# Residue-ordered copies of the normalised activations as stationary operand of six projection chunks in a hybrid decoder trunk

## Chip, cores and metric

The kernel runs on one core of one Trainium2 chip. The metric is device time in microseconds (us) of one execution; lower is better. TensorE (PE) multiplies, with its weight loads recorded apart (PEld); VectorE (DVE) and ScalarE (ACT) do elementwise work, SyncE (SP) and ACT issue the transfers.

## What is computed

One decoder layer over 512 tokens of width 1024, in float32. The part that matters here: the input is normalised (`h`, 512 x 1024), multiplied by a wide matrix `w_in`, and the product is split; among the pieces are query, key and value for three attention groups whose dilation is 1, 4 and 16:

```
h = _rms(x, norm1_w[l]) * (1 + sc1) + sh1
z, xbc, dt_raw, q, k, v, u, gates = jnp.split(h @ w_in, splits, axis=-1)
...
for gi, (win, dil) in enumerate(DILATED_GROUPS):      # ((128, 1), (512, 4), (2048, 16))
    o, lse = _dilated_window_attn(qh[:, :, sl], kh[:, :, sl], vh[:, :, sl], win // dil, dil, slopes[gi])
```

For dilations 4 and 16 the kernel wants the tokens of q, k and v grouped by their residue modulo 4: 128 tokens 0, 4, 8, ..., then 1, 5, 9, ..., and so on. After attention come a state-space branch (SSD), a pooling branch, gates, output projections and an MLP.

## The kernel before

**Number format.** Every large product is made of three: both operands are split into a high part (float32r) and a low part, and `mm3` issues low x high, high x high and high x low into the same PSUM bank (lines 285, 286, 287).

**Layout of a projection chunk.** Features lie on partitions: `hh[k]` and `hl[k]` (k = 0..7) are the high and low part of 128 features by 512 tokens. A chunk is 512 output columns of `w_in`: 8 values of k, 4 blocks j of 128 tokens, 3 products, 96 matmuls. `gemm_tok` (line 301) takes 128 tokens of `hh[k]` or `hl[k]` as the stationary operand and streams the 512 weight columns `wh`, `wl`. In the names of the profile, `psacc<-wl,hh`, the moving operand comes first and the stationary one second. Its argument `mod` selects the view of the tokens: contiguous blocks of 128, or every fourth token (`toks`, line 298). `gemm_feat` (line 289) takes the weights as the stationary operand instead and streams the tokens. `wstream` loads 512 KB of weights per two k (`raw`), splits them on ACT (`wh`, line 270) and DVE (`wl`, line 271), with three buffers each.

**First stage (lines 332 to 486).** The order on DVE, ACT, PE and SP is written out by hand. Per k: SP loads 4 blocks of the modulation matrix (`wa`) and two weight blocks (`wst`); DVE makes the modulation by dot products (line 366) and the low parts of the weights (line 385); `high(k)` scales the input (ACT line 442 and DVE line 443) and writes `hh[k]` (ACT line 446); `low(k)` writes `hl[k]` (DVE line 450); `w_high` splits weights on ACT (line 381). PE runs chunks Q and K (group 0, contiguous tokens) k by k as the operands appear. Work that follows this stage may not be placed before the two instructions `edgeV` and `edgeS`.

**Middle stage.** A scheduler orders the rest. PE runs the chunks Q+1, K+1, Q+2, K+2 (all `mod=True`), VV (`mod=False`), VV+1, VV+2 (`mod=True`), and then the `gemm_feat` chunks. Between the matmuls of these chunks stand short blocks of other PE work: transposes of q and k (lines 534, 539), scores (line 555), the exchange of softmax statistics (line 596) and the transposes of the probabilities (line 652). `take`, `take_k` and `take_v` empty the PSUM banks on ACT (line 322). In the background, DVE works off 64 further modulation dot products (line 235), whose blocks `wa` SP loads.

**Memory.** All 128 x 512 blocks come from one set of 59 slots (`blk`, `free`): a freed slot goes to the end of a queue and the next request takes its head, so a new block waits for the last reader of the old one.

Of the kernel before, what the change touches and what calls it, by code (L numbers as in the profile page):

```python
# [10 lines left out]
F32 = mybir.dt.float32  # L11
F32R = mybir.dt.float32r
AF = mybir.ActivationFunctionType
# [81 lines left out]
Z, XS, BCC, Q, K, VV, U, GS, GA, GP = 0, 2, 4, 5, 8, 11, 14, 16, 18, 20  # L95
# [3 lines left out]
def kernel(ctx: ExitStack, tc: tile.TileContext, a: dict, out: bass.AP, dbg=None):  # L99
# [16 lines left out]
    class Slots:  # L116
# [6 lines left out]
        def take(self, name, dt):  # L123
            i = self.idle.pop(0)
            t = self.pool.tile([P, T], dt, tag=f"{self.prefix}{i}", name=uid(name), bufs=1)
            self.used[id(t)] = (i, t)
            return t

        def free(self, t):
            self.idle.append(self.used.pop(id(t))[0])  # L130
# [3 lines left out]
    def blk(name, dt=F32):  # L134
        return sb.take(name, dt)
# [5 lines left out]
    def small(shape, name, bufs=1, dt=F32):  # L141
        return sm.tile(shape, dt, tag=name, name=uid(name), bufs=bufs)
# [4 lines left out]
    def acc():  # L147
        return psm("acc")
# [6 lines left out]
    V, S = nc.vector, nc.scalar  # L155
# [70 lines left out]
    def ada_load(part, k):  # L226
        wa = [blk("wa") for _ in range(2)]
        for i in range(2):
            nc.sync.dma_start(wa[i], a["w_ada"][part * 8 + k][:, i * T : (i + 1) * T])
        return wa  # L230
# [31 lines left out]
    def flush():  # L262
        while side:
            side.pop(0)()
# [9 lines left out]
    def wstream(w, nk, ch, k0=0, ahead=None):  # L274
        for kp in range(nk // 2):
            with tc.high_priority(offset=AHEAD if ahead is None else ahead):
                raw = raws.tile([P, 2, T], F32, tag="raw", name=uid("raw"))
                nc.sync.dma_start(raw, w[ch, k0 // 2 + kp])
                wh, wl = wsplit(raw, [P, 2, T])
            for i in range(2):  # L280
                yield 2 * kp + i, wh[:, i, :], wl[:, i, :]
            tick()

    def mm3(ps, wh, wl, xh, xl, first, last):
        mm(ps, lhsT=wh, rhs=xl, start=first, stop=False)  # L285
        mm(ps, lhsT=wh, rhs=xh, start=False, stop=False)  # L286
        mm(ps, lhsT=wl, rhs=xh, start=False, stop=last)  # L287
# [10 lines left out]
    def toks(t, mod):  # L298
        return t.rearrange("p (j r) -> p r j" if mod else "p (r j) -> p r j", r=4)

    def gemm_tok(w, nk, ch, ah, al, mod, ahead=None):

        ps = [acc() for _ in range(4)]
        for k, wh, wl in wstream(w, nk, ch, 0, ahead):
            th, tl = toks(ah[k], mod), toks(al[k], mod)
            for j in range(4):
                mm3(ps[j], th[:, j, :], tl[:, j, :], wh, wl, k == 0, k == nk - 1)
        return ps
# [7 lines left out]
    def evac(ps, name, func=AF.Copy):  # L316

        with tc.high_priority(offset=SOON):
            xs = [blk(name) for _ in ps]
            for x, p in zip(xs, ps):  # L320
                if func is AF.Copy:
                    S.copy(x, p)
                else:
                    S.activation(x, p, func)
        free(*ps)
        return xs

    w_in = a["w_in"]
# [3 lines left out]
    with tc.manual_schedule(engines={E.DVE, E.Activation, E.PE, E.SP}):  # L332
# [4 lines left out]
        def w_load(k):  # L337
            for ch in (Q, K):
                wt[ch, k] = blk("wst")
                nc.sync.dma_start(wt[ch, k], w_in[ch, k // 2][:, k % 2, :])  # L340
# [17 lines left out]
        A1 = [small([P, 2], f"A1{k}") for k in range(8)]  # L358
# [3 lines left out]
        def dot(k, i, half):  # L362
            if (k, i) not in dots:
                dots[k, i] = small([P, 2], "dot", 4)
            x = wa[i][half]
            V.scalar_tensor_tensor(x, x, 1.0, crow[half], ALU.mult, ALU.mult, accum_out=dots[k, i][:, half : half + 1])
            free(x)

        def dot_end(k, i):
            d, o = dots[k, i], A1[k][:, i : i + 1]  # L370
            if i == 0:
                V.scalar_tensor_tensor(o, d[:, 0:1], bsc1[:, k : k + 1], d[:, 1:2], ALU.add, ALU.add)
                V.tensor_tensor(o, o, vc("norm1_w", k), ALU.mult)
            else:
                V.scalar_tensor_tensor(o, d[:, 0:1], vc("b_ada", k), d[:, 1:2], ALU.add, ALU.add)
# [3 lines left out]
        def w_high(ch, k):  # L379
            wparts[ch, k] = blk("wsh", F32R), blk("wsl", F32R)  # L380
            S.copy(wparts[ch, k][0], wt[ch, k])

        def w_low(ch, k):
            wh, wl = wparts[ch, k]
            V.tensor_tensor(wl, wt[ch, k], wh.bitcast(F32), ALU.subtract)
            free(wt[ch, k])
# [44 lines left out]
        R1 = blk("R1")  # L431
        dot(0, 1, 1)
        dot_end(0, 1)
        hh = [cpool.tile([P, T], F32R, name=f"hh{k}", tag=f"hh{k}") for k in range(8)]
        hl = [cpool.tile([P, T], F32R, name=f"hl{k}", tag=f"hl{k}") for k in range(8)]

        us = {}

        def high(k, R):
            u = us[k] = blk("u1")  # L440
            if k:
                S.mul(u, xT[k], A1[k][:, 0:1])
                V.tensor_tensor(u, u, R, ALU.mult)
            else:
                V.scalar_tensor_tensor(u, xT[k], A1[k][:, 0:1], R, ALU.mult, ALU.mult)
            return S.activation(hh[k], u, AF.Identity, bias=A1[k][:, 1:2])

        def low(k):
            u = us.pop(k)
            i = V.scalar_tensor_tensor(hl[k], u, A1[k][:, 1:2], hh[k].bitcast(F32), ALU.add, ALU.subtract)  # L450
            free(u, xT[k])
            return i

        high(0, rp)
        w_low(Q, 0)
        S.copy(R1, rp)
# [3 lines left out]
        qps = [acc() for _ in range(4)]  # L460
        kps = [acc() for _ in range(4)]
        for k in range(8):
            if k < 7:
                wa = [ada_load(1, k + 1), ada_load(0, k + 1)]
                w_load(k + 1)
                dot(k + 1, 0, 0)
                if k:
                    low(k)
                dot(k + 1, 0, 1)
                w_high(Q, k + 1)  # L470
                w_high(K, k + 1)
                dot(k + 1, 1, 0)
                dot_end(k + 1, 0)
                dot(k + 1, 1, 1)
                w_low(Q, k + 1)
                dot_end(k + 1, 1)
                edgeS = high(k + 1, R1)
                w_low(K, k + 1)
                if k == 6:
                    edgeV = low(7)  # L480
            th, tl = toks(hh[k], False), toks(hl[k], False)
            for ch, ps in ((Q, qps), (K, kps)):
                wh, wl = wparts[ch, k]
                for j in range(4):
                    mm3(ps[j], th[:, j, :], tl[:, j, :], wh, wl, k == 0, k == 7)
                free(wh, wl)
# [16 lines left out]
    def take_k(ps):  # L503
        ks, rk = take(ps, "k")
        for tb in range(4):
            kv = ks[tb].rearrange("p (h e) -> p h e", h=4)
            with tc.high_priority(offset=SOON):
                V.tensor_tensor(kv, kv, rk[:, tb * 4 : tb * 4 + 4].unsqueeze(2).broadcast_to([P, 4, P]), ALU.mult)
        return ks

    def take_v(ps):
        return evac(ps, "v")
# [433 lines left out]
    def do(gen, n):  # L946
        side.extend([pieces(gen)] * n)

    def call(f, *args):
        side.append(lambda: f(*args))  # L950

    probs, vals, stats, pTs, oh, ol = [], [], [], [], [], []
# [22 lines left out]
    def rest(n):  # L975
        side.extend([lambda: None] * n)
# [14 lines left out]
    with tc.issue_after(edgeV.ins), tc.issue_after(edgeS.ins):  # L991
        qs, rq = take(qps, "q")
        ks = take_k(kps)
        do(ssd_steps(), 5)
        scores(0, qs, rq, ks)
        qps = gemm_tok(w_in, 8, Q + 1, hh, hl, True, 0)
    for gi in (1, 2):
        if gi > 1:
            qps = gemm_tok(w_in, 8, Q + gi, hh, hl, True)
        qs, rq = take(qps, "q")  # L1000
        kps = gemm_tok(w_in, 8, K + gi, hh, hl, True)
        ks = take_k(kps)
        flush()
        rest(gi - 1)
        scores(gi, qs, rq, ks)
    vals.append(take_v(gemm_tok(w_in, 8, VV, hh, hl, False)))
    call(do_joint)
    vals.append(take_v(gemm_tok(w_in, 8, VV + 1, hh, hl, True)))
    for h in range(4):
        call(turn_head, h)  # L1010
    vals.append(take_v(gemm_tok(w_in, 8, VV + 2, hh, hl, True)))
    for h in range(4):
        call(out_head, h)
    ps = evac(gemm_feat(w_in, 8, BCC, hh, hl), "xc")
# [177 lines left out]
    for half in range(2):  # L1192
        ah, al_ = [], []
# [81 lines left out]
```

## Time and profile before

| | us |
|---|---|
| median of 3 runs | 1121.89 (1121.78 to 1123.58) |
| the profiled execution, device time | 1121.93 |
| span of its trace (first to last instruction) | 1120.2 |
| PE busy | 1112.6 |
| DVE busy | 598.4 |
| ACT busy | 491.8 |

The profiled execution's device time is 1.7 us more than the span. A matmul's record lasts longer than the distance to the next one, since they overlap; the pace of PE is therefore read from the starts of successive matmuls, not from their durations.

### The profile page before, as it was taken

To read this page: it belongs to the slowest core of one execution; us is meant where nothing else is said; L and a number is where in the kernel's file an instruction comes from. 1 tells how busy PE (TensorE), PEld (TensorE's weight loads), DVE (VectorE), ACT (ScalarE), POOL (GpSimd) and SP (SyncE) were. 2 spreads that over 40 slices of the span, in tenths; PEclk is the share of its full clock that TensorE was granted. 3 is DMA by queue.
4 is the path that set the end of the run, shared out by engine and by line. 5 is a ranking of instruction groups with operands and counts; after the bars stand their busy time and mean duration, and the time that the engine had idled before them with its cause. 6 is when DMAs were issued, how large, how long until landed. Compare 5 with 4: busy or idle time off the path is not lost.

```text
span 1120.2 us, 14055 instructions
## 1 busy us (share of the span) xinstructions
PE 1112.6 (99%) x5414; PEld 948.4 (85%) x5414; DVE 598.4 (53%) x1210; ACT 491.8 (44%) x937; POOL 0.2 (0%) x4
## 2 busy tenths in 40 slices
PE   8999999999999999999999999999999999999998
PEld 6889998999887888888888888899888888888887
DVE  6973773582567668478833324576454233445241
ACT  5485886543497448425532123353333111344120
POOL 0000000000000000000000000000000000000000
PEclk9999999999999999999999999999999999999999
DMA  9953253334543444322333423350122322222231
GB/s 337 295 190 102 95 164 100 113 104 132 152 140 114 122 152 132 117 86 71 106 110 113 150 95 101 123 191 1 57 94 94 100 105 96 94 95 94 94 132 38
DMA packets 49347, 134.45 MB, mean 120 GB/s; under 512 B 5616, under 2 KB 6384, under 8 KB 49280
## 3 DMA queue, kind: packets, MB, share of 16 engines
q1 hardware_dynamic: 47696, 130.81, 35.5%
q10 hardware_dynamic: 1584, 2.75, 0.8%
q8 instruction: 42, 0.69, 0.3%
q14 instruction: 25, 0.20, 0.1%
HBM read 131.41 MB, written 2.13 MB: 119 GB/s over the span
## 4 chain that ended last, share of the span: by engine, by line
PE 95%; DMA 2%; ACT 2%; DVE 1%; SPq 0%; issue 0%; DVEq 0%; ACTq 0%
PE psacc L285 29%; PE psacc L287 29%; PE psacc L286 29%; PE psS L555 1%; DMA wa<-in_w_ada_dram 1%; PE psy L867 1%; PE pso L671 1%; PE psyo L875 1%; PE pso L669 1%; DVE conv L786 0%; DMA wst<-in_w_in_dram 0%; PE pskT L539 0%; PE psqT L534 0%; PE pspT L652 0%; DMA xT<-in_x_dram 0%; PE psst L827 0%
## 5 line engine op out<-in xcount | busy, mean ns | idle before, releaser
L271 DVE TENSOR_TENSOR wl<-raw,wh 128x1024 fp32r<-128x1024 f32 x161 | 197.1, 1224 | 344.4 <-ACT wh L270 342.6
L270 ACT CAST wh<-raw 128x1024 fp32r<-128x1024 f32 x161 | 168.7, 1049 | 374.5 <-PE psacc L286 323.8
L285 PE MATMUL psacc<-hl,wh 128*128 128x512 f32 x416 | 167.9, 404 | 0.5 <-ACT prev L830 0.4
L287 PE MATMUL psacc<-hh,wl 128*128 128x512 f32 x416 | 163.3, 393 | 0.0
L286 PE MATMUL psacc<-hh,wh 128*128 128x512 f32 x416 | 162.1, 390 | 0.0
L285 PE MATMUL psacc<-wl,hh 128*128 128x512 f32 x224 | 93.4, 419 | 0.0
L287 PEld LDWEIGHTS psacc<-hh,wl 128*128 128x128 f32 x416 | 78.1, 188 | 18.1
L285 PEld LDWEIGHTS psacc<-hl,wh 128*128 128x128 f32 x416 | 78.3, 188 | 17.8 <-issue 1.2
L286 PEld LDWEIGHTS psacc<-hh,wh 128*128 128x128 f32 x416 | 78.2, 188 | 17.8 <-issue 1.4
L286 PE MATMUL psacc<-ah,wh 128*128 128x512 f32 (+1 forms) x242 | 92.2, 381 | 0.0
L285 PE MATMUL psacc<-al,wh 128*128 128x512 f32 (+1 forms) x242 | 92.1, 381 | 0.0
L287 PE MATMUL psacc<-ah,wl 128*128 128x512 f32 (+1 forms) x242 | 92.1, 380 | 0.0
L286 PE MATMUL psacc<-wh,hh 128*128 128x512 f32 x224 | 90.1, 402 | 0.0
L287 PE MATMUL psacc<-wh,hl 128*128 128x512 f32 x224 | 89.7, 401 | 0.0
L285 PE MATMUL psacc<-gl,wh 128*128 128x512 f32 x224 | 88.1, 393 | 0.0
L286 PE MATMUL psacc<-gh,wh 128*128 128x512 f32 x224 | 87.5, 391 | 0.0
L287 PE MATMUL psacc<-gh,wl 128*128 128x512 f32 x224 | 87.3, 390 | 0.0
L286 PEld LDWEIGHTS psacc<-wh,hh 128*128 128x128 f32 x224 | 65.9, 294 | 1.4
L285 PEld LDWEIGHTS psacc<-wl,hh 128*128 128x128 f32 x224 | 65.4, 292 | 1.7
L287 PEld LDWEIGHTS psacc<-wh,hl 128*128 128x128 f32 x224 | 65.5, 293 | 1.5
L235 DVE SCALAR_TENSOR_TENSOR wa<-wa,crow 128x512 f32<-128x512 f32 x64 | 43.4, 688 | 22.0 <-DMA wa<-in_w_ada_dram 22.0
L286 PEld LDWEIGHTS psacc<-ah,wh 128*128 128x128 f32 x242 | 45.5, 188 | 8.8
(342 smaller groups left out, 1908.6 us busy)
## 6 DMA issues: line engine op xcount, KB each, us to landing
raw<-in_w_in_dram SPq DMA_DIRECT2D x80, 512.0 KB, 3.5
raw<-in_w_ff_dram SPq DMA_DIRECT2D x64, 512.0 KB, 3.4
wa<-in_w_ada_dram SPq DMA_DIRECT2D x96, 256.0 KB, 4.5
wst<-in_w_in_dram SPq DMA_DIRECT2D x16, 256.0 KB, 5.4
M<-prow SPq DMA_DIRECT2D x16, 256.0 KB, 3.4
raw<-in_w_ssd_out_dram SPq DMA_DIRECT2D x8, 512.0 KB, 3.5
raw<-in_w_pool_out_dram SPq DMA_DIRECT2D x8, 512.0 KB, 3.5
raw<-in_w_out_dram SPq DMA_DIRECT2D x8, 512.0 KB, 3.4
```

The lines of the kernel that those rows point to most:

```text
L235: V.scalar_tensor_tensor(wa[i], wa[i], 1.0, crow[i], ALU.mult, ALU.mult, accum_out=d[:, i : i + 1])
L270: S.copy(wh, raw)
L271: V.tensor_tensor(wl, raw, wh.bitcast(F32), ALU.subtract)
L285: mm(ps, lhsT=wh, rhs=xl, start=first, stop=False)
L286: mm(ps, lhsT=wh, rhs=xh, start=False, stop=False)
L287: mm(ps, lhsT=wl, rhs=xh, start=False, stop=last)
L555: mm(so[b], lhsT=qT[:, b * P : (b + 1) * P], rhs=kT[:, (b + 1) * P - n : (b + 1) * P], start=True, stop=True)
L669: mm(od, lhsT=vs[kb][:, hs], rhs=pT[b // 2][:, cs : cs + P], start=(b == 0), stop=False, skip_group_check=True)
L671: mm(ov[:, b, :], lhsT=vs[b][:, hs], rhs=pT[0][:, b * P : (b + 1) * P], start=False, stop=(gi == 2 and b == 3), skip_group_check=True)
L867: mm(yp[half * 64 : half * 64 + 64, cs], lhsT=X[c][:, (2 * j + half) * 64 : (2 * j + half + 1) * 64], rhs=Ms[half][:, cs], start=True, sto ...
L875: mm(op[:, cs], lhsT=prev[c][:, j * P : (j + 1) * P], rhs=CT[:, cs], start=True, stop=True)
```

## The change

Sixteen further blocks, `rh[k]` and `rl[k]`, hold copies of `hh[k]` and `hl[k]` with the tokens grouped by residue modulo 4. ACT writes them in the first stage: `rh[k]` right behind `hh[k]`, `rl[k]` behind the next k's two weight splits. The copy reads every fourth element and writes contiguously. The six chunks that took the view of every fourth token take contiguous blocks of the copies; the 16 slots are held until VV+2 is done. `edgeS` becomes the last of the copies.

```
+        rh = [blk(f"rh{k}", F32R) for k in range(8)]
+        rl = [blk(f"rl{k}", F32R) for k in range(8)]
+
+        def by_residue(part, k):
+            return S.copy(toks((rh, rl)[part][k], False), toks((hh, hl)[part][k], True).bitcast(F32))
...
-            return S.activation(hh[k], u, AF.Identity, bias=A1[k][:, 1:2])
+            S.activation(hh[k], u, AF.Identity, bias=A1[k][:, 1:2])
+            return by_residue(0, k)
...
                 w_high(Q, k + 1)
                 w_high(K, k + 1)
+                by_residue(1, k)
...
-                edgeS = high(k + 1, R1)
+                high(k + 1, R1)
                 w_low(K, k + 1)
                 if k == 6:
                     edgeV = low(7)
+                    edgeS = by_residue(1, 7)
...
-            th, tl = toks(ah[k], mod), toks(al[k], mod)
+            th, tl = toks(ah[k], False), toks(al[k], False)
...
-        qps = gemm_tok(w_in, 8, Q + 1, hh, hl, True, 0)
+        qps = gemm_tok(w_in, 8, Q + 1, rh, rl, 0)
...
-            qps = gemm_tok(w_in, 8, Q + gi, hh, hl, True)
+            qps = gemm_tok(w_in, 8, Q + gi, rh, rl)
...
-        kps = gemm_tok(w_in, 8, K + gi, hh, hl, True)
+        kps = gemm_tok(w_in, 8, K + gi, rh, rl)
...
-    vals.append(take_v(gemm_tok(w_in, 8, VV, hh, hl, False)))
+    vals.append(take_v(gemm_tok(w_in, 8, VV, hh, hl)))
...
-    vals.append(take_v(gemm_tok(w_in, 8, VV + 1, hh, hl, True)))
+    vals.append(take_v(gemm_tok(w_in, 8, VV + 1, rh, rl)))
...
-    vals.append(take_v(gemm_tok(w_in, 8, VV + 2, hh, hl, True)))
+    vals.append(take_v(gemm_tok(w_in, 8, VV + 2, rh, rl)))
+    free(*rh, *rl)
```

**First place: ACT inside the first stage.** Around k = 1, ACT's order before is this (`wsh` are high parts of weights, `u1` the scaled input):

```order
L381 CAST wsh_76_287<-wst_73_280 128x512
L381 CAST wsh_78_290<-wst_74_282 128x512
L442 ACTIVATE u1_81_300<-xT1_5_80,A11_25_126 128x512
L446 ACTIVATE hh1_242<-u1_81_300,A11_25_126 128x512
L381 CAST wsh_89_345<-wst_86_337 128x512
L381 CAST wsh_91_348<-wst_87_339 128x512
L442 ACTIVATE u1_94_358<-xT2_6_81,A12_26_127 128x512
```

And with the change, at the same place on ACT (line 443 is the copy; lines 448 and 452 are 442 and 446 of before):

```order
L381 CAST wsh_92_304<-wst_89_297 128x512
L381 CAST wsh_94_307<-wst_90_299 128x512
L443 CAST rl0_68_265<-hl0_249 128x512
L448 ACTIVATE u1_97_318<-xT1_5_80,A11_25_126 128x512
L452 ACTIVATE hh1_242<-u1_97_318,A11_25_126 128x512
L443 CAST rh1_61_258<-hh1_242 128x512
L381 CAST wsh_105_364<-wst_102_356 128x512
L381 CAST wsh_107_367<-wst_103_358 128x512
L443 CAST rl1_69_266<-hl1_250 128x512
L448 ACTIVATE u1_110_378<-xT2_6_81,A12_26_127 128x512
```

Two copies per k stand between `hh[k]` and the next k's scaling of the input, one ahead of the two weight splits and one behind them.

**Second place: ACT at the end of the first stage.** Before, three splits of the weights of Q+1 (`wh`) stand between the last `hh` and the first emptied bank (`q`):

```order
L446 ACTIVATE hh7_248<-u1_159_648,A17_31_132 128x512
L270 CAST wh_219_821<-raw_218_819 128x1024
L719 CAST wd_222_854<-wdt_221_852 128x8x16
L270 CAST wh_224_859<-raw_223_857 128x1024
L270 CAST wh_232_917<-raw_231_915 128x1024
L322 COPY q_161_706<-psacc_61_264 128x512
```

With the change, on ACT at the same place:

```order
L452 ACTIVATE hh7_248<-u1_175_678,A17_31_132 128x512
L443 CAST rh7_67_264<-hh7_248 128x512
L443 CAST rl7_75_272<-hl7_256 128x512
L270 CAST wh_235_853<-raw_234_851 128x1024
L728 CAST wd_238_886<-wdt_237_884 128x8x16
L270 CAST wh_240_891<-raw_239_889 128x1024
L322 COPY q_177_738<-psacc_77_281 128x512
```

The third split is not there any more. It stands behind the four emptied banks of q and of k and their 32 squares, in front of the square root of the keys (`rkr`, line 186):

```order
L509 ACTIVATE sqj_222_828,ssk_206_797<-k_205_792 128x128
L270 CAST wh_248_949<-raw_247_947 128x1024
L186 ACTIVATE rkr_224_831<-ssk_206_797,epsc_13_88 128x16
L270 CAST wh_257_1009<-raw_256_1007 128x1024
L270 CAST wh_299_1119<-raw_298_1117 128x1024
```

**Third place: PE in chunk VV+1.** The exchange of the softmax statistics (`psmzN`, `psmzM`, line 596, which is 605 in the changed kernel) stood here on PE, in the matmuls of k = 6:

```order
L287 MATMUL psacc_529_2171<-wh_581_2401,hl6_255 128x512
L596 MATMUL psmzN_559_2337<-exch_560_2338,toNat_558_2335 128x32
L596 MATMUL psmzN_559_2337<-exch_561_2341,toNat_558_2335 128x32
L596 MATMUL psmzN_559_2337<-exch_562_2344,toNat_558_2335 128x32
L596 MATMUL psmzN_559_2337<-exch_563_2347,toNat_558_2335 128x32
L285 MATMUL psacc_530_2172<-wl_582_2402,hh6_247 128x512
L596 MATMUL psmzM_566_2354<-exch_567_2355,toMod_565_2352 128x32
```

And with the change, on PE, it stands in those of k = 7:

```order
L286 MATMUL psacc_545_2203<-wh_597_2433,rh7_67_264 128x512
L605 MATMUL psmzN_575_2369<-exch_576_2370,toNat_574_2367 128x32
L605 MATMUL psmzN_575_2369<-exch_577_2373,toNat_574_2367 128x32
L605 MATMUL psmzN_575_2369<-exch_578_2376,toNat_574_2367 128x32
L605 MATMUL psmzN_575_2369<-exch_579_2379,toNat_574_2367 128x32
L287 MATMUL psacc_545_2203<-wh_597_2433,rl7_75_272 128x512
L605 MATMUL psmzM_582_2386<-exch_583_2387,toMod_581_2384 128x32
```

The exchange moved 11 large matmuls later; the transposes of the probabilities that need its result stand behind the same number of large matmuls as before.

## Rows read from the trace of the kernel before

**Rows 1.** The profile's page: busy time, share of the span and instructions of each engine; the clock granted to TensorE in 40 slices of the span; the chain that ended last, by engine and by line.

```profile
PE 1112.6 (99%) x5414; PEld 948.4 (85%) x5414; DVE 598.4 (53%) x1210; ACT 491.8 (44%) x937; POOL 0.2 (0%) x4
PEclk9999999999999999999999999999999999999999
PE 95%; DMA 2%; ACT 2%; DVE 1%; SPq 0%; issue 0%; DVEq 0%; ACTq 0%
```

**Rows 2.** Weight loads of the chunks Q+1, K+1, Q+2, K+2 (66.7 to 181.2 us, every fourth token), grouped by line: count, busy us, mean ns of one, idle time before them.

```profile
L286 PEld LDWEIGHTS psacc<-wh,hh 128*128 128x128 f32 x128 | 39.9, 312 | 0.0
L285 PEld LDWEIGHTS psacc<-wl,hh 128*128 128x128 f32 x129 | 39.8, 309 | 0.4
L287 PEld LDWEIGHTS psacc<-wh,hl 128*128 128x128 f32 x128 | 39.7, 310 | 0.0
```

**Rows 3.** The same for chunk VV alone (181.2 to 206.4 us, contiguous tokens).

```profile
L285 PEld LDWEIGHTS psacc<-wl,hh 128*128 128x128 f32 x32 | 6.0, 188 | 1.3
...
L287 PEld LDWEIGHTS psacc<-wh,hl 128*128 128x128 f32 x32 | 6.0, 187 | 1.5
```

**Rows 4.** Timeline of PE (start us, duration us, instruction): first and last of the 48 matmuls that open chunk Q+1 without other PE work between them.

```profile
66.81 0.40 PE L285 MATMUL psacc<-wl,hh 128*128 128x512 f32 x1
...
78.01 0.40 PE L287 MATMUL psacc<-wh,hl 128*128 128x512 f32 x1
```

**Rows 5.** Timeline of PE: first and last of the 48 matmuls that open chunk VV without other PE work between them.

```profile
181.30 0.40 PE L285 MATMUL psacc<-wl,hh 128*128 128x512 f32 x1
...
192.27 0.39 PE L287 MATMUL psacc<-wh,hl 128*128 128x512 f32 x1
```

**Rows 6.** Timeline of PE and of its weight loads in the six chunks with every fourth token, where a chunk's matmul follows other PE work: the first of 24 such places with its next two products, and the last.

```profile
88.08 0.62 PE L285 MATMUL psacc<-wl,hh 128*128 128x512 f32 x1
88.29 0.33 PEld L286 LDWEIGHTS psacc<-wh,hh 128*128 128x128 f32 x1
88.54 0.40 PE L286 MATMUL psacc<-wh,hh 128*128 128x512 f32 x1
...
258.55 0.60 PE L285 MATMUL psacc<-wl,hh 128*128 128x512 f32 x1
258.99 0.40 PE L286 MATMUL psacc<-wh,hh 128*128 128x512 f32 x1
```

**Rows 7.** Timeline of PE behind such a block in chunk VV.

```profile
200.79 0.48 PE L285 MATMUL psacc<-wl,hh 128*128 128x512 f32 x1
201.11 0.39 PE L286 MATMUL psacc<-wh,hh 128*128 128x512 f32 x1
```

**Rows 8.** Timeline of PE in a chunk of `gemm_feat`: two matmuls with 21 others of the chunk, and nothing else, between them.

```profile
284.46 0.40 PE L286 MATMUL psacc<-hh,wh 128*128 128x512 f32 x1
...
289.50 0.39 PE L287 MATMUL psacc<-hh,wl 128*128 128x512 f32 x1
```

**Rows 9.** Timeline of ACT in the first stage, one period from one scaling of the input (line 442) to the next; in brackets the idle time before, and who ended it.

```profile
29.50 0.72 ACT L442 ACTIVATE u<-xT,A 128x512 f32<-128x512 f32 x1 [1.68 <-DVE A L373]
31.45 0.73 ACT L446 ACTIVATE hh<-u,A 128x512 fp32r<-128x512 f32 x1 [1.22 <-DVE u L443]
32.07 1.13 ACT L381 CAST wsh<-wst 128x512 fp32r<-128x512 f32 x2
34.88 0.73 ACT L442 ACTIVATE u<-xT,A 128x512 f32<-128x512 f32 x1 [1.68 <-DVE A L373]
```

**Rows 10.** Timeline of DVE and PE in the first stage: DVE takes over what ACT scaled at 29.50; DVE's last `hl`; PE's first matmul that reads it.

```profile
30.72 0.69 DVE L443 TENSOR_TENSOR u<-u,R 128x512 f32<-128x512 f32 x1
...
59.08 0.75 DVE L450 SCALAR_TENSOR_TENSOR hl<-u,A,hh 128x512 fp32r<-128x512 f32 x1 [0.19 <-ACT hh L446]
...
61.67 0.39 PE L287 MATMUL psacc<-wsh,hl 128*128 128x512 f32 x1
```

**Rows 11.** Timeline of ACT and PE around the end of the first stage: the last `hh`; the first emptied banks; the last square of k; the split that follows it; PE's third pair of k in chunk Q+1.

```profile
58.33 0.72 ACT L446 ACTIVATE hh<-u,A 128x512 fp32r<-128x512 f32 x1 [1.16 <-DVE u L443]
...
64.29 0.58 ACT L322 COPY q<-psacc 128x512 f32<-128x512 f32 x1
...
75.75 0.30 ACT L500 ACTIVATE sqj<-k 128x128 f32<-128x128 f32 x1
...
76.04 1.04 ACT L270 CAST wh<-raw 128x1024 fp32r<-128x1024 f32 x1
...
77.12 1.23 DVE L271 TENSOR_TENSOR wl<-raw,wh 128x1024 fp32r<-128x1024 f32 x1 [0.77 <-ACT wh L270]
...
81.92 0.40 PE L285 MATMUL psacc<-wl,hh 128*128 128x512 f32 x1
```

**Rows 12.** Timeline of SP: the last two weight blocks of the first stage are issued; and, of ACT, the split that reads them.

```profile
40.95 1.06 SPq L340 DMA_DIRECT2D wst<-in_w_in_dram  x2
...
53.58 1.12 ACT L381 CAST wsh<-wst 128x512 fp32r<-128x512 f32 x2
```

**Rows 13.** Timeline of DVE and PE in chunk VV+1 and VV+2: DVE's last scalings of the first head's probabilities; PE's first transposes of them. Below, from the list of waits (us in total, times, longest), DVE's waits for blocks of the modulation matrix.

```profile
236.16 1.66 DVE L646 TENSOR_SCALAR p<-p,d 128x128 f32<-128x128 f32 x8
...
242.06 1.80 PE L652 MATMUL pspT<-cst,p 128*128 128x128 f32 x15
...
DVE wa L235 <- DMA wa<-in_w_ada_dram: 22.0, 19, 2.7
```

More of the change, by code (lines that the diff above doesn't have):

```diff
@@ L299, in toks, with gemm_tok @@
         return t.rearrange("p (j r) -> p r j" if mod else "p (r j) -> p r j", r=4)
-    def gemm_tok(w, nk, ch, ah, al, mod, ahead=None):
+    def gemm_tok(w, nk, ch, ah, al, ahead=None):
         ps = [acc() for _ in range(4)]
         for k, wh, wl in wstream(w, nk, ch, 0, ahead):
-            th, tl = toks(ah[k], mod), toks(al[k], mod)
+            th, tl = toks(ah[k], False), toks(al[k], False)
             for j in range(4):
```

## Prediction

> **What bounds the kernel now.** I read the page first. PE is busy for 1112.6 of the span's 1120.2 us, the clock granted to it is at its upper level (2.4 GHz) in all 40 slices, and the chain that ended last lies 95% on PE, 2% each on DMA and ACT [rows 1]. So nothing that only relieves DVE or ACT can move the end, and whatever shortens the distance between two matmuls moves it directly, as long as nobody else becomes late.
>
> Then I compared the weight loads by chunk. With every fourth token a load of 128x128 takes 309 to 312 ns [rows 2]; with contiguous tokens it takes 187 to 188 ns [rows 3]. It is the same shape and the same type; the spacing of the columns differs. The sum of the loads is not what counts, since a load runs beside the matmul before it. So I read the pace from the starts of matmuls, where 48 of them follow each other with nothing between: in Q+1 (78.01 - 66.81) / 47 = 238.3 ns [rows 4], in VV (192.27 - 181.30) / 47 = 233.4 ns [rows 5]. Of the 121 ns by which a load is shorter, 4.9 ns per matmul reach the pace.
>
> Where a chunk's matmul follows a block of other PE work, the next load has nothing to hide behind. There the second matmul starts 0.46 and 0.44 us after the first in the strided chunks [rows 6], and 0.32 us in VV [rows 7]. That is 0.12 us per place at the least, which is the difference of the two loads.
>
> **What the change removes.** Six chunks of 96 matmuls go from strided to contiguous loads: 576 matmuls. 24 of them are followed by the late load of [rows 6]; 26 are followed by a block of other work, of which I count no gain; the other 526 are ordinary steps. So 526 x 4.9 ns = 2.6 us, and 24 x 0.12 us = 2.9 us, together 5.5 us. The strided pace holds a little better over whole chunks than in the 48 of [rows 4], so I take 5.3 us. The profiled execution has 1121.93 us, of which 1120.2 are the span; the median is 1121.89. Thus 1121.9 - 5.3 = 1116.6 us, if the rest costs nothing.
>
> **What it adds: 16 copies on ACT.** No copy that reads every fourth element stands in the trace. From below, a cast of 128x512 on ACT takes 0.56 us (1.13 for two) [rows 9]. From above, I scale by the loads of [rows 2, 3], 310 / 188 = 1.65, which gives 0.92 us. I take 0.6 to 0.9 us. Two copies per k then cost 1.2 to 1.8 us. ACT's period in the first stage is 34.88 - 29.50 = 5.38 us, of which it idles 1.68 us before line 442 and 1.22 us before line 446 [rows 9]; both pauses end with DVE. The first copy (`rh`) and the second (`rl`) both lie in the first pause, around the two weight splits. They fit up to 0.84 us each without moving line 442. Above that, 442 is late, but its result, begun at 29.50 and done at 30.22, is taken up by DVE only at 30.72 [rows 9, 10]: another 0.5 us, so up to about 1.1 us per copy the first stage does not stretch at all. Beyond it, the stage has a reserve at its end: DVE's last `hl` is done at 59.08 + 0.75 = 59.83 us, and PE reads it at 61.67 [rows 10], 1.8 us later. What queues behind a late copy on ACT is line 442, then 443 on DVE, then `hh` and `hl`, then PE.
>
> **Slots and transfers.** The 16 new blocks leave 16 fewer free slots, so the last weight loads of the first stage have to wait until PE gives blocks back. The last one is issued from 40.95 to 42.01 us, and ACT splits what it brings at 53.58 [rows 12]: 11.6 us apart. The wait I estimate at under 1 us from the order of the freed blocks, and a transfer may be late by several before it shows. Cost nothing.
>
> **The moved third split.** After `hh7` (58.33 + 0.72) the two last copies stand on ACT; `rl7` needs `hl7` (59.83) and ends at 60.4 to 60.8. Two splits of 1.04 us follow, so ACT is at the emptying of `q` by about 63 us, and before that emptying began at 64.29, when PE had finished the bank [rows 11]. Nothing lost. The third split now follows the last square of k (75.75 + 0.30), about where the next split stood (76.04), and its low part, 1.23 us on DVE after about a microsecond of delay, is done at about 78.5 [rows 11]. PE wants that pair at 81.92, now at 81.92 - 0.24 = 81.7: some 3 us remain. This cover would be gone if the emptying of banks slid by 3 us.
>
> **Chunk VV+1.** The exchange of the statistics moves 11 large matmuls back, 11 x 0.235 = 2.6 us, while the first transposes of the probabilities stay at their place. Between the two, DVE scales the first head's probabilities: the eight of before start at 236.16 and end at 237.82, and PE asks for them at 242.06 [rows 13]. Of these 4.2 us the exchange takes 2.6; about 1 more goes because PE arrives earlier (five of the six chunks are behind it, but all work that leads here moves with it, so only VV+1's part counts: 0.2 to 0.7 us). One 1.14 us low part that now stands between the scalings takes most of the rest. I come out at 0 to 1 us of reserve, so I expect no wait, but it is the tightest place. If a block for one of the modulation dots is late too, DVE waits up to 2.7 us [rows 13], and PE would stand for 1 to 2.5 us.
>
> **The rivals.**
>
> (a) *Part is given back in VV+1.* The wait just described costs 2.5 us at the most: 1116.6 + 2.5 = 1119.1. For it: the thin reserve. Against it: the transposes of the first head are 15 in a block of 1.80 us [rows 13], and only the last four read the last scalings.
>
> (b) *Nothing changes, since the column spacing is not what the loads pay for.* Then loads stay at 310 ns behind contiguous copies and the time is 1121.9. What could do it instead: the six chunks differ from VV in which tiles they run beside. Against it: the first stage and VV, contiguous, lie on both sides of the strided ones in time, and VV stands between K+2 and VV+1 with the same `hh` and `hl`. The Trainium skill has a rule on this side (TensorE: Matmul & The Clock Gate, "LDWEIGHTS (loading the stationary operand)"): the time of a load goes by its number of columns alone. The trace disagrees, 309 against 188 ns for the same 128 columns [rows 2, 3].
>
> (c) *Slower: the copies are far dearer than 0.92 us and stretch the first stage.* One mechanism: ACT's period becomes 5.38 - 1.68 - 1.22 + 2c plus the 1.22 that DVE still takes between 442 and 446, less the 0.5 of DVE's slack: 2c + 3.2. Above c = 1.1 us, DVE and then PE run at that period for 7 values of k; PE loses 7 x 2 x (c - 1.1) less the 1.8 of reserve. The whole gain is gone at c = 1.6 us; it is slower by more than 0.2% (2.2 us, about what a measurement of this kernel can tell from no change) from 1.75 us, and with c = 2 us it would be 1116.6 + 12.6 - 1.8 = 1127.4. For it: no such copy is in the trace. Against it: 1.75 us is three times the contiguous cast, and the loads pay 1.65 times [rows 2, 3, 9]. A rule of the Trainium skill speaks against the change here (SBUF — State Buffer, "Door 1: The DMA port swizzle (why `[64,N]` ≈ `[32,N]`)"): SBUF has lines of 16 bytes, and an access that goes to a new line pays a penalty, which a copy that reads every fourth float32 does at each element. It gives no figure for ACT; if ACT pays as the loads of [rows 2] do, the copy is the 0.92 us of above and costs the end nothing, and without the penalty it would be 0.56 and cost nothing either; only a penalty of three times makes this rival.
>
> (d) *More than forecast: the pace falls to that of `gemm_feat`.* There the steps are (289.50 - 284.46) / 22 = 229.1 ns [rows 8], also with contiguous loads. 526 x (233.4 - 229.1) = 2.3 us more, so 1114.3. Against it: VV, with the same order of operands as the six chunks, runs at 233.4.
>
> **How the numbers follow.** Forecast (1116.6; its own range 1115.5 to 1118.0, from 4.7 ns to 5.2 ns per step, 0.10 to 0.13 us per place, and a few gains at the 26 places I left out, against a wait of up to 1 us in VV+1): 0.68. (a) 1119.1: 0.13. (b) 1121.9: 0.06. (c) 1127: 0.05. (d) 1114.3: 0.06. A remaining 0.02 is for something slow that I don't see. Faster by over 0.2% means below 1119.65: forecast, (d) and most of (a), 0.84; within 0.2%: (b) and the tail of (a), 0.09; slower: 0.07. The range leaves out (b), (c) and (d): 1115.3 to 1119.6.
>
> **What would show it.** Right: loads of the six chunks near 188 ns, 48 undisturbed matmuls of Q+1 in 47 x 233.4 ns, 0.32 us behind other work, the first stage ending at 66.6 as before, and no new PE wait in VV+1. The copies' duration shows whether ACT had room: under 1.1 us. Wrong: loads still at 310 (b); line 442 begun later each k and PE waiting for `hl` in the first stage (c); PE idle before the transposes of VV+1 (a), or before the third pair of Q+1, which I priced at nothing.

## The result, and the profile after

The changed kernel takes 1115.51 us (median of 4 runs, 1114.45 to 1116.29) against 1122.11 us for the kernel before in runs beside it. The ratio is 0.9938 with a 95% interval of 0.9922 to 0.9954; on the scale of the prediction (1121.89 us) that is 1114.9 us. The change gains 7.0 us where 5.3 were forecast, and 1114.9 lies just under 1115.3, the lower end of the range. The profiled execution took 1115.78 us, its span is 1114.0 us.

The page of the changed kernel, to be held against [rows 1]: busy time by engine, granted clock, and the chain that ended last.

```profile
PE 1104.2 (99%) x5414; PEld 916.2 (82%) x5414; DVE 597.5 (54%) x1210; ACT 507.4 (46%) x953; POOL 0.2 (0%) x4
PEclk9999999999999999999999999999999999999999
PE 91%; DMA 3%; ACT 3%; DVE 2%; issue 1%; SPq 0%; ACTq 0%; DVEq 0%
```

PE is still the bound, at the upper clock throughout. PEld fell by 32 us, ACT grew by 15.6. The weight loads of the six chunks, grouped as in [rows 2] (first four chunks), and those of VV as in [rows 3]:

```profile
L286 PEld LDWEIGHTS psacc<-wh,rh 128*128 128x128 f32 x128 | 24.1, 188 | 4.7
L285 PEld LDWEIGHTS psacc<-wl,rh 128*128 128x128 f32 x128 | 24.1, 188 | 5.3 <-ACT qT L544 0.5
...
L286 PEld LDWEIGHTS psacc<-wh,hh 128*128 128x128 f32 x32 | 6.0, 188 | 1.3
```

The loads are now 188 ns, just like VV's. The pace is not. The timeline of PE: first and last of the 48 matmuls that open Q+1 [rows 4], a place behind other work [rows 6], and the 48 that open VV [rows 5].

```profile
66.78 0.40 PE L285 MATMUL psacc<-wl,rh 128*128 128x512 f32 x1
...
77.47 0.39 PE L287 MATMUL psacc<-wh,rl 128*128 128x512 f32 x1
...
87.27 0.50 PE L285 MATMUL psacc<-wl,rh 128*128 128x512 f32 x1
87.61 0.40 PE L286 MATMUL psacc<-wh,rh 128*128 128x512 f32 x1
...
176.86 0.40 PE L285 MATMUL psacc<-wl,hh 128*128 128x512 f32 x1
...
187.83 0.40 PE L287 MATMUL psacc<-wh,hl 128*128 128x512 f32 x1
```

Q+1 takes (77.47 - 66.78) / 47 = 227.4 ns per step, VV still (187.83 - 176.86) / 47 = 233.4 ns. Both load contiguous blocks in 188 ns and stream the same kind of weights; only the stationary tile differs, `rh`, `rl` here and `hh`, `hl` there.

**Where the time went.** The chunks are counted in PE's order from 0, so that the six are 2 to 5, 7 and 8, VV is 6 and the first of `gemm_feat` is 9. From the first matmul of Q+1 to the first of the `gemm_feat` chunks it is 199.82 us before (66.81 to 266.63) and 192.49 us after (66.78 to 259.27): 7.33 us gained. In the six chunks, the 550 steps from one large matmul to the next took 135.62 us before and 127.96 after, 7.66 us less; the blocks between them took 0.33 us more. The regular steps among them fell from 238.2 to 228.4 ns on average, and not to 227: in the trace some ten steps of 224 to 240 ns follow each block before the pace settles at 226 to 227 ns. Of the 7.33 us, 1.2 are given back up to the start of chunk 15, and over the 690 us from there to the end both kernels agree within 0.02 us. That leaves 6.2 us between the two profiled executions; the 7.0 us come from all fast runs, among which the profiled one of the changed kernel was not the fastest.

**The copies.** The timeline of ACT in the first stage, to be held against [rows 9], and DVE's take-over of the scaled input [rows 10]:

```profile
28.87 1.14 ACT L443 CAST rl<-hl 128x512 fp32r<-128x512 f32 x1
29.91 0.72 ACT L448 ACTIVATE u<-xT,A 128x512 f32<-128x512 f32 x1
31.42 0.72 ACT L452 ACTIVATE hh<-u,A 128x512 fp32r<-128x512 f32 x1 [0.78 <-DVE u L449]
32.18 1.13 ACT L443 CAST rh<-hh 128x512 fp32r<-128x512 f32 x1
33.21 1.14 ACT L381 CAST wsh<-wst 128x512 fp32r<-128x512 f32 x2
34.26 1.12 ACT L443 CAST rl<-hl 128x512 fp32r<-128x512 f32 x1
35.27 0.73 ACT L448 ACTIVATE u<-xT,A 128x512 f32<-128x512 f32 x1
```

```profile
30.70 0.69 DVE L449 TENSOR_TENSOR u<-u,R 128x512 f32<-128x512 f32 x1
```

A copy takes 1.12 us, 1.01 to 1.04 from start to start. The pause of 1.68 us before the scaling is gone. The scaling starts 0.41 us later than before (29.50), but DVE takes it up at 30.70 as before, the period is 5.36 us, and the first stage ends where it did, 66.78 against 66.81 us.

### The profile page after: what moved, and what is told of

Same layout as the page of the kernel before. It is cut to its first block, busy times and chain, and to the rows that moved or that the text cites. A ratio compares the mean times of both kernels' runs of the same rounds, so it can differ in the third digit from the quotient of the medians.

```text
span 1114.0 us, 14077 instructions
## 1 busy us (share of the span) xinstructions
PE 1104.2 (99%) x5414; PEld 916.2 (82%) x5414; DVE 597.5 (54%) x1210; ACT 507.4 (46%) x953; POOL 0.2 (0%) x4
## 4 chain that ended last, share of the span: by engine, by line
PE 91%; DMA 3%; ACT 3%; DVE 2%; issue 1%; SPq 0%; ACTq 0%; DVEq 0%
PE psacc L285 28%; PE psacc L287 28%; PE psacc L286 28%; DMA wa<-in_w_ada_dram 1%; PE psS L564 1%; DMA M<-prow 1%; PE psy L876 1%; ACT wh L270 1%; DVE conv L795 1%; PE psyo L884 1%; PE pskT L548 0%; DMA wst<-in_w_in_dram 0%; PE psqT L543 0%; PE pspT L661 0%; DMA xT<-in_x_dram 0%
## 5 line engine op out<-in xcount | busy, mean ns | idle before, releaser
L285 PE MATMUL psacc<-wl,rh 128*128 128x512 f32 x192 | 77.1, 402 | 0.0
L287 PE MATMUL psacc<-wh,rl 128*128 128x512 f32 x192 | 75.2, 393 | 0.0
L286 PE MATMUL psacc<-wh,rh 128*128 128x512 f32 x192 | 75.0, 390 | 0.0
L285 PEld LDWEIGHTS psacc<-al,wh 128*128 128x128 f32 x242 | 45.5, 188 | 8.8
L287 PEld LDWEIGHTS psacc<-ah,wl 128*128 128x128 f32 x242 | 45.5, 188 | 8.8
L287 PEld LDWEIGHTS psacc<-gh,wl 128*128 128x128 f32 x224 | 42.0, 188 | 9.7
```

## Experiments

A fact of the memory layout that the compiled program shows, for what follows: in each partition `hh` and `hl` start at bytes 17824 to 48544, 32 bytes past a multiple of 128. The weights (`wh` from byte 77408) and all slots, with them the copies (`rh0` at 161376), start 96 bytes past one. The place modulo 128 is called the residue below, and the difference of two residues their distance.

**Contiguous loads without copies.**

```
-            th, tl = toks(ah[k], mod), toks(al[k], mod)
+            th, tl = toks(ah[k], False), toks(al[k], False)
```

> The kernel before, whose six chunks take contiguous blocks of 128 tokens of hh and hl themselves; no copies, and the order on every engine is that of before. (The regrouping of the tokens by residue is left out, so q, k and v of groups 1 and 2 hold other tokens.) This is the price of contiguity as the prediction counted it. Theory PLACE (the pace of contiguous loads depends on where the stationary tile lies in memory; hh and hl start 32 bytes past a multiple of 128, the copies and the weights 96 bytes past one): the six chunks run at 233.4 ns per step like VV, 1116.6 us, 1.1 us or more above the changed kernel. Rival CHUNK (VV is slow for a reason of its own, and the six run at 228 from any contiguous tile): 228 ns, and 1114.6 to 1115.5 us.

Measured: 1117.45 us, ratio 0.9955 (0.994 to 0.997), 5.0 us gained. Timeline of PE, the 48 that open Q+1:

```profile
66.61 0.39 PE L285 MATMUL psacc<-wl,hh 128*128 128x512 f32 x1
...
77.57 0.40 PE L287 MATMUL psacc<-wh,hl 128*128 128x512 f32 x1
```

That is 233.2 ns per step, VV's pace, in the chunks that run at 227 from the copies. The gain is what the prediction had counted, in size too (5.3 us). So CHUNK fell, and the place of the tile matters.

**VV from the copies.**

```
-    vals.append(take_v(gemm_tok(w_in, 8, VV, hh, hl)))
+    vals.append(take_v(gemm_tok(w_in, 8, VV, rh, rl)))
```

> The changed kernel, whose chunk VV takes rh and rl too (so that v of group 0 holds other tokens); order as in the changed kernel. PLACE, by residue or by region: VV falls from 233.3 to 227 or 228 ns per step, 0.5 us for 91 steps. CHUNK: VV stays at 233.3 ns.

Measured: 1114.63 us, ratio 0.9931 (0.9916 to 0.9946). Timeline of PE, the 48 that open VV:

```profile
176.51 0.39 PE L285 MATMUL psacc<-wl,rh 128*128 128x512 f32 x1
...
187.16 0.40 PE L287 MATMUL psacc<-wh,rl 128*128 128x512 f32 x1
```

226.6 ns: the same chunk, with nothing else changed, is 6.8 ns per step faster from the other tiles.

**hh and hl moved by 64 bytes.**

```
+        cpool.tile([P, 16], F32, name="pad0", tag="pad0")
         hh = [cpool.tile([P, T], F32R, name=f"hh{k}", tag=f"hh{k}") for k in range(8)]
         hl = [cpool.tile([P, T], F32R, name=f"hl{k}", tag=f"hl{k}") for k in range(8)]
+        cpool.tile([P, 16], F32, name="pad1", tag="pad1")
```

> The changed kernel with 64 unused bytes ahead of hh and 64 behind hl: hh and hl now start 96 bytes past a multiple of 128, as the copies and the weights do; all else keeps its residue modulo 128 and its order. PLACE by the residue: the first stage (from about 30 us) and VV fall from 233.3 to 227 or 228 ns per step, some 250 steps of 5.5 ns, 1.4 us, so 1114.1 us or less. Rival PLACE by region (low addresses are slow, not the residue) and rival CHUNK: 233.3 ns there as before and 1115.5 us.

Measured: 1109.73 us, ratio 0.9887 (0.9872 to 0.9902). Timeline of PE: the last 96 matmuls of the first stage (k = 4 to 7 of Q and K), and the 48 that open VV.

```profile
43.91 0.39 PE L285 MATMUL psacc<-wsl,hh 128*128 128x512 f32 x1
...
65.44 0.39 PE L287 MATMUL psacc<-wsh,hl 128*128 128x512 f32 x1
...
175.62 0.39 PE L285 MATMUL psacc<-wl,hh 128*128 128x512 f32 x1
...
186.27 0.39 PE L287 MATMUL psacc<-wh,hl 128*128 128x512 f32 x1
```

226.6 ns in both, down from 233.3. The region is the same, so it is the residue. The gain is 5.8 us and not the 1.4 that I had worked out: the chunks that *stream* `hh` and `hl` (and later `gh`, `gl`, in the same memory) gained too. One of them, the second of `gemm_feat`, goes from 229.0 ns per regular step before to 227.3.

**Which residue.** The same pads in other sizes. "All at 32" puts 64 bytes behind `hl` only, "all at 0" 96 ahead and 64 behind; "hh at 64" 32 and 96, "hh at 0" 96 and 32.

> The changed kernel with 64 unused bytes behind hl: hh and hl stay 32 bytes past a multiple of 128, and the weights, the copies and all other large blocks move from 96 to 32 as well. Theory SAME (a step is short when stationary and moving operand start at the same residue modulo 128): 227 ns per step in the first stage, in VV and in the six chunks, and about 1109.7 us as with hh shifted by 64. Rival OWN (the stationary operand's own residue counts, 96 is good and 32 bad): 233 ns wherever the stationary operand is, thus in the later chunks too; 4000 steps of 5 to 6 ns more, about 1133 us.

> The changed kernel with 32 unused bytes ahead of hh and 96 behind hl: hh and hl start at a multiple of 64 (64 past a multiple of 128), all else at 96. SAME: the first stage and VV stay at 233 ns per step, the six chunks at 228; 1115.5 us. OWN: open, since 64 was not seen; 233 at worst.

> The changed kernel with 96 unused bytes ahead of hh and 32 behind hl: hh and hl start at a multiple of 128, all else at 96. SAME: 233 ns in the first stage and VV, 1115.5 us, as with 64. OWN: open. If it is the distance modulo 64 that counts (32 in this run and in the one with 64), both differ from the changed kernel, where that distance is 64.

> The changed kernel with 96 unused bytes ahead of hh and 64 behind hl: all large blocks start at a multiple of 128. SAME: 227 ns per step everywhere and about 1109.7 us. OWN: open; if multiples of 128 were better than 96, below 227 ns in all chunks, 4000 steps, at most some 13 ns each down to the 213 ns of 512 columns at 2.4 GHz.

Measured, with the mean of the regular steps of VV and of the second `gemm_feat` chunk (weights stationary, `hh` and `hl` streamed):

| kernel | weights minus hh, modulo 128 | VV, ns | gemm_feat, ns | us | ratio (interval) |
|---|---|---|---|---|---|
| changed | 64 | 233.3 | 229.0 | 1115.51 | 0.9938 (0.9922 to 0.9954) |
| hh shifted by 64 | 0 | 227.2 | 227.3 | 1109.73 | 0.9887 (0.9872 to 0.9902) |
| all at 32 | 0 | 227.3 | 227.3 | 1109.24 | 0.9887 (0.987 to 0.9903) |
| all at 0 | 0 | 227.1 | 227.4 | 1109.89 | 0.9889 (0.9875 to 0.9904) |
| hh at 64 | 32 | 233.3 | 233.2 | 1121.94 | 0.9998 (0.9989 to 1.0007) |
| hh at 0 | 96 | 233.2 | 233.3 | 1121.2 | 0.9994 (0.9985 to 1.0003) |

(The `gemm_feat` figure of the changed kernel is that of its second profile, below.) Timelines of PE, the 48 that open VV: first "hh at 64", then "all at 32", then "all at 0".

```profile
178.04 0.39 PE L285 MATMUL psacc<-wl,hh 128*128 128x512 f32 x1
...
189.01 0.39 PE L287 MATMUL psacc<-wh,hl 128*128 128x512 f32 x1
```

```profile
175.48 0.39 PE L285 MATMUL psacc<-wl,hh 128*128 128x512 f32 x1
...
186.13 0.40 PE L287 MATMUL psacc<-wh,hl 128*128 128x512 f32 x1
```

```profile
176.79 0.39 PE L285 MATMUL psacc<-wl,hh 128*128 128x512 f32 x1
...
187.44 0.39 PE L287 MATMUL psacc<-wh,hl 128*128 128x512 f32 x1
```

233.4 against 226.6 ns in both others. SAME stands: with stationary and streamed operand at one residue modulo 128 the pace is 227 whether that residue is 0, 32 or 96; at distances of 32, 64 and 96 VV is at 233. OWN falls, since 32 is good when all are at 32. My 1115.5 us for "hh at 64" and "hh at 0" was 6 us too low: at these distances the later chunks that stream `hh` slow down as well, from 229 to 233 ns, and the whole gain of the change is gone. Why the distance matters is not shown, and the modulus is open too. In the three padded layouts that run at 227 the weights lie 59648 bytes behind `hh`, which is 233 x 256, and the copies lie a multiple of 256 bytes from the weights as well; the slow distances of 64, 32 and 96 are 192, 32 and 224 modulo 256. A distance of 128 bytes was in no run, so 256 fits as well as 128.

**Stride and place apart.** Plain copies, in the same slots, and the old view of them:

```
-            return S.copy(toks((rh, rl)[part][k], False), toks((hh, hl)[part][k], True).bitcast(F32))
+            return S.copy((rh, rl)[part][k], (hh, hl)[part][k].bitcast(F32))
...
-        qps = gemm_tok(w_in, 8, Q + 1, rh, rl, 0)
+        qps = gemm_tok(w_in, 8, Q + 1, rh, rl, 0, True)
...
```

> The changed kernel with plain copies of hh and hl (no regrouping in the copy) in the same slots; the six chunks read every fourth token of them. Order as in the changed kernel. Copies cost 0.56 us each instead of 1.12. If place and stride add up: loads stay at 310 ns, and the pace is 238 less some 5, about 233 ns per step; 1119 us. If stride alone sets the strided pace: 238 ns per step, and 1121.9 us, the copies and the 16 slots being worth nothing in themselves.

Measured: 1120.25 us, ratio 0.9983 (0.9973 to 0.9992), and 235.5 ns per regular step. A row of the grouped weight loads of Q+1, and ACT's copies (ns: least, median, most; first and last start).

```profile
L286 PEld LDWEIGHTS psacc<-wh,rh 128*128 128x128 f32 x32 | 9.9, 310 | 0.0
```

```profile
L443 ACT CAST rh<-hh x8: 621/622/625, 20.3 to 58.8; 128x512 fp32r<-128x512 f32 x8
```

The regular step of the six chunks in the four combinations: 238.2 ns (strided, `hh`), 233.6 (contiguous, `hh`), 235.5 (strided, slots), 228.4 (contiguous, slots). Stride and place do not simply add up: the place gives 2.7 ns to strided loads and 5.2 to contiguous ones. The plain copy takes 0.62 us, the regrouping one 1.12. So on ACT too a read of every fourth float32 is dearer, 1.8 times. The Trainium skill (SBUF — State Buffer, "Door 1: The DMA port swizzle (why `[64,N]` ≈ `[32,N]`)") lets each access to a new line of 16 bytes pay; that agrees with the copies, and with loads of 310 against 188 ns.

**Only the pads, without the change.** The kernel before, with the two pads of 64 bytes shown above.

> The kernel before (no copies, every fourth token of hh and hl) with 64 unused bytes ahead of hh and 64 behind hl, so that hh and hl start at the residue of the weights modulo 128. By theory SAME: the six chunks at 235.4 ns per step as from copies in slots, 526 steps of 2.7 ns, 1.4 us; the first stage and VV at 227, 250 steps of 6.6 ns, 1.6 us; and the later chunks that stream hh, hl, gh or gl from 229 to 227 ns, about 4 us by the difference of the changed kernel and its shifted form. Together about 1115 us, so 128 unused bytes would be worth as much as the whole change. If the place helps only contiguous loads: the six chunks stay at 238 ns and it is 1116.4 us.

Measured: 1115.65 us, ratio 0.9945 (0.993 to 0.996). The six chunks run at 235.5 ns, as forecast. 128 unused bytes are worth nearly as much as the change (6.2 against 7.0 us, with intervals that overlap), and both together 12.7 us (hh shifted by 64, above: 0.0113 x 1121.89).

**Only the costs.** Copies and slots as in the change, the chunks reading `hh` and `hl` as before.

> The changed kernel with its 16 copies and 16 slots as they are, but the six chunks read every fourth token of hh and hl as in the kernel before; nobody reads the copies. This is the price of what the change adds. If ACT hides the copies, as the prediction has it: 1121.9 us, PE's first stage ending at 66.6 us. If they or the slots cost something that the gain covers up: above 1122.5 us.

Measured: 1121.95 us, ratio 0.9999 (0.9989 to 1.0008). The 16 copies, the 16 slots and the moved work cost nothing that the interval of some 1 us would show, at the pace of before.

**A third copy per k.**

```
                 by_residue(1, k)
+                by_residue(1, k)
```

> The changed kernel in which ACT writes rl[k] twice for k = 0 to 6: a third copy per k in the same pause. In the changed kernel a copy takes 1.04 us from start to start, and between the scaling on ACT and DVE that takes it up some 0.15 us are left. If that pause is used up (the copies stood at the edge of their cover): 0.9 us later per k, 6.2 us over the seven, less the 1.8 us by which DVE leads at the end: the first stage ends 4 to 5 us later, 1119 to 1120.5 us. If there is room left elsewhere on ACT: 1115.5 us, no change.

Measured: 1126.08 us, ratio 1.0033 (1.002 to 1.0046). Timeline of ACT, one period of the first stage; PE's waits; and a table by stretch (span, busy us and count of PE, PEld, DVE, ACT and POOL, granted clock, DMA share, GB/s).

```profile
31.88 0.72 ACT L448 ACTIVATE u<-xT,A 128x512 f32<-128x512 f32 x1
...
38.35 0.72 ACT L448 ACTIVATE u<-xT,A 128x512 f32<-128x512 f32 x1
```

```profile
PE psdtT L746 <- ACT dT L741: 2.8, 1, 2.8
```

```profile
85.00:92.00 7.00, 6.84 (x20) 5.32 (x20) 6.21 (x16) 3.22 (x4) 0.00 (x0) 0.55 0.76 231
92.00:130.00 38.00, 38.00 (x182) 31.60 (x181) 15.33 (x38) 20.31 (x57) 0.00 (x0) 1.00 0.27 95
```

The period is 38.35 - 31.88 = 6.47 us instead of 5.36, and the first stage ends 5.8 us later (72.58 against 66.78). That is more than the 4 to 5 expected, since each period grew by 1.11 us and not by 0.9. The expected total, 1119 to 1120.5 us, was missed by some 6 us, and most of that comes behind the stage: ACT, whose order behind the stage shifts a little, is late with `dT`, PE stands for 2.8 us, and then the granted clock is 0.55 over 85 to 92 us, with 13 matmuls at about 427 ns, 13 x 0.2 = 2.6 us. The three make 5.8 + 2.8 + 2.6 = 11.2 us. Up to chunk 9 the kernel is 11.3 us behind the changed one (270.54 against 259.27), and up to chunk 15 some 0.9 of it comes back, which leaves about the 10.6 us between the medians. The changed kernel itself stands about 0.1 us per k from this cliff: its scaling is done at 29.91 + 0.72 = 30.63 us, and DVE takes it up at 30.70.

**The changed kernel once more.**

> The changed kernel once more, unchanged. In its first profile PE waited 0.74 us for DVE's ol behind a late block of the modulation matrix in chunk 10, and 0.4 us more than before for prev. If that is the change's doing, it stands here again; if it hangs on the moment at which a transfer lands, it is gone, and this profile is 0.9 us or more shorter than the first. Time 1114.6 to 1115.6 us.

Measured: 1114.45 us (1114.25 to 1116.85), ratio 0.9934 (0.9917 to 0.995). The profiled execution is the slowest of the four, 1.07 us longer than the first profile and not 0.9 us shorter. That lies ahead of everything the change touches. PE stood 2.84 us early in the first stage (2.76 in the first profile). Behind that, by the table by stretch, the granted clock was 0.89 and then 0.68 over 8 to 16 us, where the first profile has 1.00, and chunk Q+1 starts at 68.18 instead of 66.78 us:

```profile
9.73 0.70 PE L404 MATMUL pssx<-sq,ones 128*128 128x512 f32 x1 [2.84 <-DVE sq L403]
...
8.00:12.00 4.00, 2.26 (x4) 0.69 (x5) 2.16 (x4) 3.97 (x9) 0.00 (x0) 0.89 1.03 388
12.00:16.00 4.00, 4.00 (x7) 1.78 (x7) 1.76 (x6) 0.34 (x1) 0.00 (x0) 0.68 1.05 389
...
68.18 0.40 PE L285 MATMUL psacc<-wl,rh 128*128 128x512 f32 x1
```

So the two profiles are compared by their waits and not by their length. PE's waits behind chunk 9, first in the first profile of the changed kernel, then in this one:

```profile
PE psacc L285 <- ACT prev L839: 0.8, 1, 0.8
PE psacc L285 <- DVE ol L313: 0.7, 1, 0.7
```

```profile
PE psacc L285 <- ACT prev L839: 1.5, 1, 1.5
```

The wait for `ol` is gone. In the first profile it went back to DVE, which had waited 3.06 us for a block of the modulation matrix ahead of the convolution that ACT and then `ol` wait for:

```profile
290.29 0.69 DVE L235 SCALAR_TENSOR_TENSOR wa<-wa,crow 128x512 f32<-128x512 f32 x1 [3.06 <-DMA wa<-in_w_ada_dram]
...
297.56 0.51 PE L285 MATMUL psacc<-hl,wh 128*128 128x512 f32 x1 [0.74 <-DVE ol L313]
```

So this one hung on a transfer. The wait for `prev` (0.4 us in the kernel before) is larger instead. Up to chunk 15 the changed kernel gives back 1.2 us in the one and 1.0 us in the other execution, and nothing with VV from the copies, in the same order of instructions. So a give-back of about 1 us stands in both profiles of the changed kernel, with its parts in different places; what sets it is open.

## Why the prediction was wrong

- **The pace of the contiguous copies is the step that failed.** It took VV's 233.4 ns [rows 5] for the six chunks: 526 x 4.9 ns = 2.6 us. Measured are 228.4 ns, a term of about 5.2 us; the range had allowed 4.7 to 5.2 ns per step, and it was 9.8. The reason given against rival (d), that VV has the same order of operands, was true and did not bear on it: VV's stationary tiles lie at another residue modulo 128 than the weights, the copies at the same. The run without copies gives what the prediction counted: 233.6 ns and 5.0 us. So what was predicted of contiguity held, and the rest came from the place of the copies, which the prediction did not look at. Rival (d) came nearest, with 229.1 ns and 1114.3 us at a chance of 0.06, but it named the form of `gemm_feat` and not the place. The trace before had a sign of it, in two stretches of `gemm_feat` chunks with the weights stationary. The first streams `ah`, `al` out of slots (residue 96, as the weights), the second `gh`, `gl` in the memory of `hh`, `hl` (residue 32). Below are the first and last of 96 matmuls without other work between them:

```profile
864.85 0.39 PE L285 MATMUL psacc<-al,wh 128*128 128x512 f32 x1
...
886.38 0.39 PE L287 MATMUL psacc<-ah,wl 128*128 128x512 f32 x1
```

```profile
799.02 0.39 PE L285 MATMUL psacc<-gl,wh 128*128 128x512 f32 x1
...
820.77 0.39 PE L287 MATMUL psacc<-gh,wl 128*128 128x512 f32 x1
```

  That is 226.6 against 228.9 ns per step, in one kernel and one form of chunk.
- **Behind other work**, 24 x 0.12 us = 2.9 us were predicted. These steps took 10.30 us before (24 steps) and 7.59 us after (23, since one has become a regular step), 0.43 and 0.33 us each; in the row at 87.27 it is 0.34 us against the 0.32 assumed. That is 24 x 0.10 = 2.4 us: right in kind, 0.5 us too much in size.
- **The 26 places that end on a block** were counted as nothing: 6.58 us before, 6.59 after. Right.
- **The copy** was put at 0.6 to 0.9 us and took 1.12, more than the 0.92 taken as its upper bound. The term was undersized, but the limit of 1.1 us per copy that the prediction worked out for the first stage agrees with what the third copy shows. It was hidden, as said, but nearer to the edge than said.
- **Slots, transfers, third split**: nothing, as predicted (0.9999 for the costs alone). The last two weight blocks of the first stage were issued 1.9 us later than in [rows 12], where under 1 us was estimated, still far ahead of the split that reads them:

```profile
42.81 0.80 SPq L340 DMA_DIRECT2D wst<-in_w_in_dram  x2
```

  The third pair of Q+1 started at 81.36 without a wait; DVE had its low part ready at 78.94.
- **VV+1**: a reserve of 0 to 1 us was forecast, and no wait. The first head's scalings and PE's transposes, against [rows 13]:

```profile
233.22 1.46 DVE L655 TENSOR_SCALAR p<-p,d 128x128 f32<-128x128 f32 x7
...
235.72 1.80 PE L661 MATMUL pspT<-cst,p 128*128 128x128 f32 x15
```

  235.72 - 234.68 = 1.04 us are left, and PE does not wait. Right.
- **Not foreseen**: up to 1.2 us given back from chunk 10 to 14, in the waits for `ol` and `prev` above, of which the kernel before has only 0.4 us for `prev`. It is partly luck that the time lies so near the range: this loss, counted as nothing, covers half of what the pace gave beyond the forecast.

Together: 7.7 us less in the six chunks where 5.3 were forecast, 0.3 more in the blocks, up to 1.2 given back; 6.2 us in the profile, 7.0 by the ratio.

## What to carry to other kernels

A pace that is borrowed from another chunk belongs to its tiles, not to the form of its instructions: look at where both operands start before it is put into a sum. Look whether tiles that meet in one matmul start a multiple of 256 bytes apart, which was the fast case here (whether 128 would do was not run); two pads of 64 bytes gave nearly as much as sixteen copies. And where a pause hides new work, work out how much of it is left: with one copy more per k the time went from 7 us faster to 4 us slower.

## What the runs showed that was not expected

- With 128 contiguous token columns stationary and 512 weight columns streamed, matmuls follow each other at 226.6 ns when both operands start a multiple of 256 bytes apart, and at 233.4 ns when the distance modulo 256 is 32, 192 or 224; the loads take 188 ns in both cases (changed kernel).
- At a distance of 64 (modulo 128), chunks that stream `hh` against stationary weights can settle at either pace: the second `gemm_feat` chunk ran at 229.0 ns per step in the second profile of the changed kernel and at 233.1 in that of the unused copies.
- A copy on ACT that reads every fourth float32 takes 1.12 us, a plain one 0.62.
- In the run with a third copy PE stood 2.8 us, and behind it the granted clock was at its lower level for 13 matmuls (427 instead of 227 ns). A pause of about this length did not always do it: in the first stage PE stood 2.76 us in one profile of the changed kernel and 2.84 us in the other, and only in the second was the granted clock lower behind it; what decides is open.
